# Splitting a modulation vector's sums between TensorE and VectorE at the start of a two-block transformer kernel

## The chip, the cores and the metric

One core of one Trainium2 chip runs the whole program. The metric is the device time of one execution in microseconds, as a median over runs; times within the program are counted from the first instruction of the profiled execution.

## What is computed

The reference runs two blocks of two layers each over 256 positions of width 1024. What matters here is its very beginning:

```python
c_act = jax.nn.silu(c)                                   # (1, 1024)
mod = c_act @ ada_w[l] + ada_b[l]                        # (1, 6144): six vectors of 1024
sh1, sc1, g1, sh2, sc2, g2 = jnp.split(mod, 6, axis=-1)
h = rmsnorm(x, norm_mix[l]) * (1.0 + sc1) + sh1
proj = h @ w_in[l]                                       # columns 512 to 1024 (a_v) are computed first
```

Nothing of the first layer's projection can begin before `sc1` and `sh1` are there, and each of them is a product of a vector of 1024 with a matrix of 1024 x 1024 (4 MB in float32). The rest (the mixer, a retrieval feed-forward network, a second block) follows from `h`.

## The kernel before

The inputs are float32. A projection's operands are each split into a rounded part `hi` and a difference `lo`, and three TensorE products of them are added. ScalarE makes `hi` (line 153), VectorE makes `lo` (line 154, recorded under its helper, line 81).

`first_norm` (line 745) makes `h` for the first layer. The matrix rows for `sc1` (group 1) and then `sh1` (group 0) come in 8 chunks each of 128 rows x 1024 columns, 512 KB, numbered 0 to 15 in this text. A ring of 7 buffers takes them: two tiles `ada_raw` and five slices of `more`. Each `part` (line 267) issues one transfer on SP's queue and one VectorE instruction that multiplies the chunk by one element of `cact` per partition and adds it to `ada_acc` (line 279 for a group's first chunk, line 282 for the others). Each `fin` (line 284) then adds up the partitions on TensorE, with `ada_acc` as the stationary operand and a column of ones moving:

```python
for j in range(8):
    pe.matmul(ps[:, j:j + 1], lhsT=st[g][:, j * 128:j * 128 + 128], rhs=ones, start=True, stop=True)
store = lambda: tt(MOD[l][:, g * 8:g * 8 + 8], ps[:, 0:8], C("ada_b", l * 48 + g * 8, 8), ALU.add)
```

The profile records each of these matmuls as two passes. I call the 16 passes of 8 such matmuls a set.

Meanwhile ScalarE takes the sums of squares of `X` (line 204), VectorE makes the reciprocal roots, ScalarE scales the rows (`xn`, line 760), and TensorE transposes them into four PSUM banks (`turn`, line 396, recorded at line 223). When both groups are there, ScalarE turns the banks into `hT_hi` with scale and shift (line 417), 8 instructions; VectorE (line 434) and, for the second half, ScalarE (line 432) make the full value `hfull`, and VectorE takes `hT_lo` from it (line 436). I call this the turn. The first projection starts on it: `Lead.rounded` (line 568) multiplies the first six rows of 128 of the weights, for which three weight chunks of 512 KB (two rows of 128 each) are loaded and split beforehand, chunks 0 and 1 ahead of the turn and chunk 2 in it. `Lead.small` (line 574) and `proj_half` (line 602) follow.

Within `first_norm` the orders of TensorE, VectorE and ScalarE are those in which the program is written (`tc.manual_schedule`). SP's queue issues transfers in order: a transfer into a ring buffer waits until the buffer's last reader is done, and all transfers behind it wait with it.

Of the kernel before, what the change touches and what calls it, by code (L numbers as in the profile page):

```python
# [8 lines left out]
F32 = mybir.dt.float32  # L9
F32R = mybir.dt.float32r  # L10
# [37 lines left out]
def kernel(ctx: ExitStack, tc: tile.TileContext, x, cols, ada_w, w_in, gm_wt, gm_vnorm, w_out,  # L48
# [214 lines left out]
    def ada_tasks(l, groups, acc, ring=None, name="ada", late=None, late_groups=(), halved=False, fetched=None):  # L263
        tasks = []
        st = {"n": 0}

        def part(g, k):
            src = ada_source(l, g, k)
            if fetched:
                raw = fetched(l, g, k)  # L270
            elif ring:
                raw = ring[st["n"] % len(ring)]
                st["n"] += 1
                sy.dma_start(raw, src)
            else:
                raw = load(src)
            if k == 0:
                st[g] = acc(g)
                ts(st[g], raw, cact[:, 0:1], None, ALU.mult)
                return  # L280
            for c in [slice(0, 512), slice(512, 1024)] if halved else [slice(0, 1024)]:
                ve.scalar_tensor_tensor(st[g][:, c], raw[:, c], cact[:, k:k + 1], st[g][:, c], ALU.mult, ALU.add)

        def fin(g):
            ps = bank("ta" if g in late_groups else name)
# [3 lines that stand above are left out]
            if g in late_groups:  # L289
                return store  # L290
            store()

        for g in groups:
            for k in range(8):
                tasks.append(lambda g=g, k=k: part(g, k))
            (late if g in late_groups else tasks).append(lambda g=g: fin(g))
        return tasks
# [79 lines left out]
    class Norm:  # L377
# [38 lines left out]
                else:  # L416
                    se.activation(d, src, AF.Identity, bias=self.shift[:, k:k + 1], scale=g)

        def lo(self, t, q):
            hi, lo = self.hT  # L420
            p = self.pieces(t)[4 * q:4 * q + 4]
            if self.shift is None:
                for k, src, c in p:
                    ve.scalar_tensor_tensor(lo[:, k, c], src, self.g[:, k:k + 1], hi[:, k, c].bitcast(F32), ALU.mult, ALU.subtract)
                return
            n = 4 if self.apart else 2
            for i in range(0, len(p), n):
                w = self.scr.tile([128, 512], F32, name="hfull", tag="hfull", bufs=1)
                for j, (k, src, c) in enumerate(p[i:i + n]):
                    d = w[:, j * 512 // n:(j + 1) * 512 // n]  # L430
                    if q:
                        se.activation(d, src, AF.Identity, bias=self.shift[:, k:k + 1], scale=self.g[:, k:k + 1])
                    else:
                        ts(d, src, self.g[:, k:k + 1], self.shift[:, k:k + 1], ALU.mult, ALU.add)
                d, c = slice(4 * q + i, 4 * q + i + n), p[i][2]
                tt(lo[:, d, c], w.rearrange("p (a b) -> p a b", a=n), hi[:, d, c].bitcast(F32), ALU.subtract)
# [308 lines left out]
    def first_norm(scr, hT, acc, ring):  # L745

        E = mybir.EngineType
        n = Norm(scr, lambda: gain1(0, 1, "norm_mix", "g_mix"), MOD[0][:, 0:8])
        n.hT = hT
        tasks = ada_tasks(0, (1, 0), acc, ring, "ta")  # L750
        src = paired(w_in[0, :, 512:1024])
        with tc.manual_schedule(engines={E.PE, E.DVE, E.Activation}):
            tasks[0]()
            for t in range(T):
                x_sumsq(t, X[:, t, :], strm.tile([128, 1024], F32, name="junk", tag="raw", bufs=3))
            r = rsqrt(sums[:, :, 0, 0], T, 1.0 / D)
            for t in range(T):
                parts[t] = [None, 0, None]
                xn = strm.tile([128, D], F32, name="xn", tag="raw", bufs=3)
                se.activation(xn, X[:, t, :], AF.Copy, scale=r[:, t:t + 1])  # L760
                n.turn(xn, t)
            for f in tasks[1:8] + tasks[9:12] + tasks[8:9]:
                f()
            n.prepare(0)
            for f in tasks[12:17]:
                f()
            ws = halves(0, src(0)) + halves(1, src(1))
            tasks[17]()
            for t in range(T):
                n.hi(t)  # L770
            n.lo(1, 0)
            ws += halves(2, src(2))
            n.lo(1, 1)
            cur["lead"] = ld = Lead(hT, ws, "sv", 1)
            for t in range(T):
                ld.parts(t)
            for i in range(len(ws)):
                for t in range(T):
                    ld.rounded(t, i)
            for t in range(T):  # L780
                ld.small(t)
# [927 lines left out]
```

## Time and profile before

| | us |
|---|---|
| runs | 2322.08, 2322.60, 2324.01 |
| median | 2322.6 |
| profiled execution, its own time | 2323.63 |
| its span, first to last instruction | 2321.8 |
| TensorE busy in the span | 2255.4 (97%) |
| VectorE busy | 1760.9 (76%) |
| ScalarE busy | 1198.8 (52%) |

The profiled execution is 1.0 us above the median, and 1.8 us of its time lie outside the span. The shares are means over the whole program; the stage in question is the first 36 us, 1.6% of it, in which the shares are others. PE is TensorE's matmul row and PEld its loading of stationary operands, DVE is VectorE, ACT is ScalarE, SP the queue that issues the transfers.

### The profile page before, as it was taken

The numbers are of one execution on the slowest core, as the hardware profiler recorded it, in microseconds if no ns is written. First come the engines' busy times: TensorE is split into PE (matmuls) and PEld (weight loads), VectorE is DVE, ScalarE is ACT, GpSimd is POOL, SyncE is SP. The second block draws the span as 40 slices with busy tenths as digits, with TensorE's granted clock in tenths as the row PEclk, the third lists the DMA queues.
The fourth block names the chain that finished last, engine by engine and source line by source line (L and its number), as shares of the span: only waits on it lengthen the run. The fifth ranks groups of instructions, "written<-read, shape, count | busy, mean of one in ns | idle before, by whom it ended". The sixth has DMA issues, their size and how long they took to land.

```text
span 2321.8 us, 39096 instructions
## 1 busy us (share of the span) xinstructions
PE 2255.4 (97%) x14953; PEld 2017.1 (87%) x14953; DVE 1760.9 (76%) x3277; ACT 1198.8 (52%) x1925; POOL 12.3 (1%) x36
## 2 busy tenths in 40 slices
PE   5999999999999999999999999999999999999998
PEld 4889999999887888888999999998888877987796
DVE  7875999999867777656489899996755666577556
ACT  4655545554444445466445555545444554654454
POOL 0000000000000000000000000000000000000000
PEclk8999999999999999999999999999999999999999
DMA  8845655544588887543455554447666673443552
GB/s 320 272 144 162 184 180 173 160 152 153 171 273 289 280 294 220 169 150 118 155 157 182 182 157 162 150 149 230 224 186 189 199 226 104 130 135 117 175 154 82
DMA packets 122029, 424.12 MB, mean 183 GB/s; under 512 B 14433, under 2 KB 15841, under 8 KB 121842
## 3 DMA queue, kind: packets, MB, share of 16 engines
q1 hardware_dynamic: 121842, 421.63, 57.2%
q8 instruction: 117, 1.92, 0.3%
q14 instruction: 70, 0.57, 0.1%
HBM read 420.53 MB, written 1.05 MB: 182 GB/s over the span
## 4 chain that ended last, share of the span: by engine, by line
PE 82%; DVE 10%; DMA 3%; ACT 2%; issue 2%; SPq 0%; DVEq 0%; ACTq 0%; POOL 0%
PE op L1048 10%; PE op L1050 9%; PE op L1049 9%; PE up L228 9%; PE up L230 9%; PE up L229 9%; DVE lo L81 3%; PE pc L230 3%; PE pc L228 3%; PE pc L229 3%; DVE Wx L81 2%; PE gg L958 2%; PE op L238 1%; PE op L241 1%; PE op L239 1%
## 5 line engine op out<-in xcount | busy, mean ns | idle before, releaser
L81 DVE TENSOR_TENSOR lo<-raw,hi 128x1024 fp32r<-128x1024 f32 x686 | 835.6, 1222 | 326.4 <-ACT hi L153 325.2
L153 ACT ACTIVATE hi<-raw 128x1024 fp32r<-128x1024 f32 x686 | 720.1, 1052 | 266.0 <-PE pc L229 75.5
L230 PE MATMUL up<-hT_hi,lo 128*128 128x256 f32 x2048 | 580.9, 284 | 5.0 <-DVE lo L81 4.8
L228 PE MATMUL up<-hT_hi,hi 128*128 128x256 f32 x2048 | 585.0, 286 | 0.0
L229 PE MATMUL up<-hT_lo,hi 128*128 128x256 f32 x2048 | 579.2, 283 | 0.0
L230 PEld LDWEIGHTS up<-hT_hi,lo 128*128 128x128 f32 x2048 | 392.4, 192 | 8.5 <-DVE lo L81 8.3
L229 PEld LDWEIGHTS up<-hT_lo,hi 128*128 128x128 f32 x2048 | 392.7, 192 | 0.0
L228 PEld LDWEIGHTS up<-hT_hi,hi 128*128 128x128 f32 x2048 | 392.3, 192 | 0.0
L1050 PE MATMUL op<-hi,lo 128*128 128x512 f32 x976 | 385.6, 395 | 2.7 <-DVE lo L81 2.7
L1048 PE MATMUL op<-hi 128*128 128x512 f32 x976 | 386.2, 396 | 0.2
L1049 PE MATMUL op<-lo,hi 128*128 128x512 f32 x976 | 385.2, 395 | 0.0
L1050 PEld LDWEIGHTS op<-hi,lo 128*128 128x128 f32 x976 | 183.0, 187 | 49.1 <-DVE lo L81 4.6
L1048 PEld LDWEIGHTS op<-hi 128*128 128x128 f32 x976 | 183.0, 188 | 45.0 <-DVE Wx L81 1.1
L1049 PEld LDWEIGHTS op<-lo,hi 128*128 128x128 f32 x976 | 183.0, 188 | 44.3
L228 PE MATMUL pc<-hT_hi,hi 128*128 128x256 f32 x568 | 160.9, 284 | 0.4 <-ACT hi L153 0.4
L230 PE MATMUL pc<-hT_hi,lo 128*128 128x256 f32 x568 | 160.7, 284 | 0.4 <-DVE lo L81 0.2
L229 PE MATMUL pc<-hT_lo,hi 128*128 128x256 f32 x568 | 160.7, 283 | 0.0
L990 ACT ACTIVATE up<-up 128x256 f32<-128x256 f32 (+31 forms) x140 | 37.7, 269 | 207.1 <-PE up L230 199.6
L153 ACT ACTIVATE hi<-Wy 128x256 fp32r<-128x256 f32 x120 | 50.1, 418 | 162.2 <-PE op L1049 162.1
L993 ACT ACTIVATE Wy<-up 128x256 f32<-128x256 f32 (+1 forms) x120 | 46.2, 385 | 167.1 <-PE up L230 167.0
L153 ACT ACTIVATE hi<-Wx 128x256 fp32r<-128x256 f32 x124 | 51.2, 415 | 129.2 <-PE op L1049 123.3
L228 PEld LDWEIGHTS pc<-hT_hi,hi 128*128 128x128 f32 x568 | 108.9, 192 | 1.4 <-ACT hi L153 1.3
(437 smaller groups left out, 3136.0 us busy)
## 6 DMA issues: line engine op xcount, KB each, us to landing
raw<-in_peer_ut_dram SPq DMA_DIRECT2D x256, 512.0 KB, 3.7
raw<-in_peer_v_dram SPq DMA_DIRECT2D x256, 512.0 KB, 4.3
Wx<-in_ada_w_dram SPq DMA_DIRECT2D x56, 512.0 KB, 5.5
raw<-in_even_w_dram SPq DMA_DIRECT2D x42, 512.0 KB, 4.1
raw<-in_w_in_dram SPq DMA_DIRECT2D x40, 512.0 KB, 4.4
raw<-in_peer_wq_dram SPq DMA_DIRECT2D x32, 512.0 KB, 4.0
raw<-in_odd_w_in_dram SPq DMA_DIRECT2D x32, 512.0 KB, 4.4
ada_raw<-in_ada_w_dram SPq DMA_DIRECT2D x30, 512.0 KB, 5.2
```

The costliest lines, as they stand in the source:

```text
L81: return ve.tensor_tensor(out, a, b, op)
L153: se.activation(hi, raw, AF.Copy)
L228: pe.matmul(dst, lhsT=wh[:, c0:c0 + 128], rhs=hh[:, k, :], start=first, stop=False, skip_group_check=True)
L229: pe.matmul(dst, lhsT=wh[:, c0:c0 + 128], rhs=hl[:, k, :], start=False, stop=False, skip_group_check=True)
L230: pe.matmul(dst, lhsT=wl[:, c0:c0 + 128], rhs=hh[:, k, :], start=False, stop=last, skip_group_check=True)
L238: pe.matmul(d, lhsT=a, rhs=wh[:, g * n:g * n + n], start=first, stop=False, **mk)
L958: pe.matmul(ps[:, a, q * 128:q * 128 + 128], lhsT=B[:, n // 2, :, n % 2], rhs=side[:, n // 2, :, n % 2], start=side is A and q == 0, stop= ...
L990: se.activation(ps[:, :P], ps[:, :P], AF.Gelu_apprx_tanh)
L993: se.activation(row(b)[:, P:], ps[:, P:256], AF.Gelu_apprx_tanh)
L1048: pe.matmul(d, lhsT=a, rhs=vh[:, s], start=first, stop=False, **mk)
L1049: pe.matmul(d, lhsT=a, rhs=vl[:, s], start=False, stop=False, **mk)
L1050: pe.matmul(d, lhsT=c, rhs=vh[:, s], start=False, stop=last, **mk)
```

## The change

Only `first_norm` and an argument of `Norm.lo` change. Chunks with an odd number within their group are multiplied on TensorE directly, with the chunk as the stationary operand and one column of `cact` moving, into the group's PSUM bank, where the products add up. Chunks with an even number are summed on VectorE as before, and after the sixth chunk of a group their sum goes into the same bank by `ones`. The `mod` addition comes when chunk 7 of the group has been multiplied. A ring buffer is filled again when its chunk has been used, by either engine.

The transposes stand after chunk 3's use. The first weight chunk is requested after chunk 6's use, that is between the requests for chunks 13 and 14; the other two after chunk 14's. Weight chunk 0 is split ahead of the turn, chunks 1 and 2 within it.

```diff
--- before.py
+++ after.py
@@ -416,7 +416,7 @@
                 else:
                     se.activation(d, src, AF.Identity, bias=self.shift[:, k:k + 1], scale=g)
 
-        def lo(self, t, q):
+        def lo(self, t, q, only=None):
             hi, lo = self.hT
             p = self.pieces(t)[4 * q:4 * q + 4]
             if self.shift is None:
@@ -424,7 +424,7 @@
                     ve.scalar_tensor_tensor(lo[:, k, c], src, self.g[:, k:k + 1], hi[:, k, c].bitcast(F32), ALU.mult, ALU.subtract)
                 return
             n = 4 if self.apart else 2
-            for i in range(0, len(p), n):
+            for i in range(0, len(p), n) if only is None else only:
                 w = self.scr.tile([128, 512], F32, name="hfull", tag="hfull", bufs=1)
                 for j, (k, src, c) in enumerate(p[i:i + n]):
                     d = w[:, j * 512 // n:(j + 1) * 512 // n]
@@ -747,30 +747,89 @@
         E = mybir.EngineType
         n = Norm(scr, lambda: gain1(0, 1, "norm_mix", "g_mix"), MOD[0][:, 0:8])
         n.hT = hT
-        tasks = ada_tasks(0, (1, 0), acc, ring, "ta")
-        src = paired(w_in[0, :, 512:1024])
+        order = [(g, k) for g in (1, 0) for k in range(8)]
+        src = lambda kk: w_in[0, kk * 256:kk * 256 + 256, 512:1024].rearrange("(a p) c -> p a c", p=128)
+        banks, sum_of = {}, {}
+
+        def fetch(m):
+            if m < len(order):
+                sy.dma_start(ring[m % len(ring)], ada_source(0, *order[m]))
+
+        def products(g, lhs, rhs, last):
+
+            first = g not in banks
+            if first:
+                banks[g] = bank("ta")
+            for j in range(8):
+                pe.matmul(banks[g][:, j:j + 1], lhsT=lhs[:, j * 128:j * 128 + 128], rhs=rhs, start=first and j == 0,
+                          stop=last, skip_group_check=True)
+
+        def use(m):
+
+            g, k = order[m]
+            raw = ring[m % len(ring)]
+            if k % 2:
+                products(g, raw, cact[:, k:k + 1], k == 7)
+            elif k == 0:
+                sum_of[g] = acc(g)
+                ts(sum_of[g], raw, cact[:, 0:1], None, ALU.mult)
+            else:
+                ve.scalar_tensor_tensor(sum_of[g], raw, cact[:, k:k + 1], sum_of[g], ALU.mult, ALU.add)
+                if k == 6:
+                    products(g, sum_of[g], ones, False)
+            fetch(m + len(ring))
+            if k == 7:
+                tt(MOD[0][:, g * 8:g * 8 + 8], banks[g][:, 0:8], C("ada_b", g * 8, 8), ALU.add)
+
+        def rounded(raw):
+            hi = strm.tile([128, 1024], F32R, name="hi", tag="hi")
+            se.activation(hi, raw, AF.Copy)
+            return hi
+
+        def rest(raw, hi):
+            lo = strm.tile([128, 1024], F32R, name="lo", tag="lo")
+            tt(lo, raw, hi.bitcast(F32), ALU.subtract)
+            return lo
+
         with tc.manual_schedule(engines={E.PE, E.DVE, E.Activation}):
-            tasks[0]()
+            for m in range(len(ring)):
+                fetch(m)
+            use(0)
             for t in range(T):
                 x_sumsq(t, X[:, t, :], strm.tile([128, 1024], F32, name="junk", tag="raw", bufs=3))
             r = rsqrt(sums[:, :, 0, 0], T, 1.0 / D)
+            for m in (1, 2, 3):
+                use(m)
             for t in range(T):
                 parts[t] = [None, 0, None]
                 xn = strm.tile([128, D], F32, name="xn", tag="raw", bufs=3)
                 se.activation(xn, X[:, t, :], AF.Copy, scale=r[:, t:t + 1])
                 n.turn(xn, t)
-            for f in tasks[1:8] + tasks[9:12] + tasks[8:9]:
-                f()
-            n.prepare(0)
-            for f in tasks[12:17]:
-                f()
-            ws = halves(0, src(0)) + halves(1, src(1))
-            tasks[17]()
-            for t in range(T):
-                n.hi(t)
-            n.lo(1, 0)
-            ws += halves(2, src(2))
+            for m in (4, 5, 6):
+                use(m)
+            raw0 = load(src(0), (128, 2, 512))
+            for m in range(7, 15):
+                use(m)
+                if m == 8:
+                    n.prepare(0)
+            raw1 = load(src(1), (128, 2, 512))
+            hi0 = rounded(raw0)
+            lo0 = rest(raw0, hi0)
+            use(15)
+            p = n.pieces(1)
+            turn_hi = lambda a, b: [se.activation(n.hT[0][:, k, c], ps, AF.Identity, bias=n.shift[:, k:k + 1],
+                                                  scale=n.g[:, k:k + 1]) for k, ps, c in p[a:b]]
+            turn_hi(0, 4)
+            n.lo(1, 0, (0,))
+            hi1 = rounded(raw1)
+            turn_hi(4, 8)
+            lo1 = rest(raw1, hi1)
+            raw2 = load(src(2), (128, 2, 512))
+            hi2 = rounded(raw2)
+            n.lo(1, 0, (2,))
+            lo2 = rest(raw2, hi2)
             n.lo(1, 1)
+            ws = halves(0, (hi0, lo0)) + halves(1, (hi1, lo1)) + halves(2, (hi2, lo2))
             cur["lead"] = ld = Lead(hT, ws, "sv", 1)
             for t in range(T):
                 ld.parts(t)
```

What this does to TensorE's queue, from its start (`ta` is a group's bank, `tp` the bank of a transpose, `sv` that of the first projection):

```order
+L764 MATMUL ta<-cact,ada_raw_109 128x1 x8
+L764 MATMUL ta<-cact,more 128x1 x8
 L223 MATMUL tp<-ident,xn 128x128 x16
-L287 MATMUL ta<-ones,ada_acc 128x1 x16
+L764 MATMUL ta<-cact,more 128x1 x8
+L764 MATMUL ta<-ones,ada_acc 128x1 x8
+L764 MATMUL ta<-cact,ada_raw_108 128x1 x8
+L764 MATMUL ta<-cact,more 128x1 x24
+L764 MATMUL ta<-ones,ada_acc 128x1 x8
+L764 MATMUL ta<-cact,ada_raw_109 128x1 x8
 L571 MATMUL sv<-hi,hT_hi 128x512
```

Where two reductions of 8 matmuls stood between the transposes and the first projection, there are now 80 matmuls, 16 of them ahead of the transposes.

VectorE's queue behind the reciprocal roots:

```order
-L282 SCALAR_TENSOR_TENSOR ada_acc<-ada_raw_109,cact,ada_acc 128x1024
-L282 SCALAR_TENSOR_TENSOR ada_acc<-more,cact,ada_acc 128x1024 x5
-L282 SCALAR_TENSOR_TENSOR ada_acc<-ada_raw_108,cact,ada_acc 128x1024
+L777 SCALAR_TENSOR_TENSOR ada_acc<-more,cact,ada_acc 128x1024 x3
+L81 TENSOR_TENSOR mod_101<-ta,col 128x8
 L85 TENSOR_SCALAR ada_acc<-ada_raw_109,cact 128x1024
-L282 SCALAR_TENSOR_TENSOR ada_acc<-more,cact,ada_acc 128x1024 x2
+L311 SCALAR_TENSOR_TENSOR g_mix<-mod_101,col 128x8
+L777 SCALAR_TENSOR_TENSOR ada_acc<-more,cact,ada_acc 128x1024 x2
+L777 SCALAR_TENSOR_TENSOR ada_acc<-ada_raw_108,cact,ada_acc 128x1024
```

The seven sums of the first group become three, and the addition that makes `mod` from TensorE's bank now stands ahead of the second group's first chunk.

ScalarE's queue around the turn (`hT_hi` is the turn, `hi<-raw` the rounding of a weight chunk):

```order
-L153 ACTIVATE hi<-raw 128x1024 x2
-L417 ACTIVATE hT_hi<-tp,mod_101,g_mix 128x256 x8
-L153 ACTIVATE hi<-raw 128x1024
+L786 ACTIVATE hi<-raw 128x1024
+L820 ACTIVATE hT_hi<-tp,mod_101,g_mix 128x256 x4
+L786 ACTIVATE hi<-raw 128x1024
+L820 ACTIVATE hT_hi<-tp,mod_101,g_mix 128x256 x4
+L786 ACTIVATE hi<-raw 128x1024
 L432 ACTIVATE hfull<-tp,mod_101,g_mix 128x256 x4
```

One rounding has moved from ahead of the turn into its middle.

## Rows read from the trace of the kernel before

**Rows 1.** The page, busy time by engine: us, share of the span, instructions.

```profile
PE 2255.4 (97%) x14953; PEld 2017.1 (87%) x14953; DVE 1760.9 (76%) x3277; ACT 1198.8 (52%) x1925; POOL 12.3 (1%) x36
```

**Rows 2.** The chain of waits, 8 to 37 us: start, us, what.

```profile
20.35 1.30 DVE ada_acc L282
...
21.69 3.59 PE ta L287 x16
...
30.86 1.30 DVE ada_acc L282
...
32.20 3.59 PE ta L287 x16
...
36.01 0.57 ACT hT_hi L417
```

**Rows 3.** Busy time by stretch; last three columns granted TensorE clock, DMA share, GB/s.

```profile
12.50:21.60 9.10, 3.65 (x16) 3.28 (x16) 8.88 (x9) 2.19 (x2) 0.00 (x0) 0.98 1.01 390
...
25.30:32.10 6.80, 0.00 (x0) 0.00 (x0) 6.62 (x8) 2.08 (x2) 0.00 (x0) 0.50 0.98 351
```

**Rows 4.** Timeline of TensorE: start, us, instruction; transposes and one-column passes.

```profile
13.84 3.65 PE L223 MATMUL tp<-ident,xn 128*128 128x128 f32 x16 [13.84 <-ACT xn L760]
...
147.50 1.03 PE L223 MATMUL tp<-ident,xn 128*128 128x128 f32 x8
...
149.75 3.63 PE L287 MATMUL ta<-ones,ada_acc 128*128 128x1 f32 x32
...
154.80 1.97 PE L223 MATMUL tp<-ident,xn 128*128 128x128 f32 x8 [1.42 <-DVE xn L85]
```

**Rows 5.** Busy time by stretch (as rows 3: PE, PEld, DVE, ACT, POOL, clock, DMA, GB/s).

```profile
21.70:25.20 3.50, 3.50 (x16) 3.48 (x16) 3.17 (x3) 0.00 (x0) 0.00 (x0) 0.50 1.02 376
32.20:35.70 3.50, 3.50 (x16) 3.49 (x16) 2.22 (x2) 0.00 (x0) 0.00 (x0) 0.50 0.67 207
35.80:41.60 5.80, 4.97 (x12) 3.91 (x13) 5.21 (x10) 5.11 (x10) 0.00 (x0) 0.50 0.99 395
...
149.80:153.30 3.50, 3.50 (x33) 3.49 (x31) 2.39 (x9) 0.72 (x2) 0.00 (x0) 1.00 0.36 136
...
154.50:157.70 3.20, 2.90 (x14) 2.90 (x15) 2.00 (x8) 2.18 (x5) 0.00 (x0) 0.50 0.00 0
```

**Rows 6.** SP's issues of chunks 1 and 14, 15, with chunks 1 and 15 to landing.

```profile
2.66 0.43 SPq L274 DMA_DIRECT2D ada_raw<-in_ada_w_dram  x1
...
ada_raw<-in_ada_w_dram SPq DMA_DIRECT2D x1, 512.0 KB, 7.3
...
21.66 0.99 SPq L274 DMA_DIRECT2D ada_raw<-in_ada_w_dram  x2
...
ada_raw<-in_ada_w_dram SPq DMA_DIRECT2D x1, 512.0 KB, 6.0
```

**Rows 7.** Timeline of ScalarE: the scaled rows and the turn.

```profile
12.55 2.19 ACT L760 ACTIVATE xn<-X,rs_y 128x1024 f32<-128x1024 f32 x2 [4.94 <-DVE rs_y L131]
...
36.01 3.75 ACT L417 ACTIVATE hT_hi<-tp,mod,g_mix 128x256 fp32r<-128x256 f32 x8 [3.88 <-DVE mod L81]
```

**Rows 8.** Timeline of VectorE: differences of weight chunks, and its part of the turn.

```profile
32.06 2.35 DVE L81 TENSOR_TENSOR lo<-raw,hi 128x1024 fp32r<-128x1024 f32 x2
...
37.07 0.99 DVE L86 TENSOR_SCALAR hfull<-tp,g_mix,mod 128x256 f32<-128x256 f32 x2 [0.43 <-ACT hT_hi L417]
38.10 0.69 DVE L81 TENSOR_TENSOR hT_lo<-hfull,hT_hi 128x512 fp32r<-128x512 f32 x1
```

**Rows 9.** The chain of waits, first projection: one matmul's step early and later.

```profile
40.41 0.43 PE sv L571
...
42.24 0.23 PE sv L572
```

**Rows 10.** Busy time by stretch after the stage (columns as rows 3).

```profile
44.80:60.00 15.20, 14.53 (x95) 12.70 (x94) 11.25 (x14) 9.34 (x10) 0.00 (x0) 1.00 0.89 294
60.00:100.00 40.00, 39.48 (x258) 34.91 (x257) 32.79 (x54) 26.26 (x33) 0.00 (x0) 1.00 0.84 283
100.00:150.00 50.00, 49.48 (x278) 41.95 (x277) 42.35 (x96) 30.11 (x47) 0.00 (x0) 1.00 0.56 190
```

## The prediction

> **What bounds the kernel now.** Over the whole span TensorE is the bound [rows 1], but the change lies in the first 36 us, before the projections begin, so I read that stage by itself, first in the chain of waits. There the links are VectorE's modulation sums, one per chunk at 1.30 us, then a reduction of 16 TensorE passes (8 matmuls by `ones`, two passes each) of 3.59 us, twice, and after the second (32.20 + 3.59 = 35.79 us) ScalarE's turn of the activations begins at 36.01 [rows 2]. 35.79 is the time that the change must beat.
>
> Next, what stands beside that chain. In the two stretches of sums VectorE is busy 8.88 of 9.10 and 6.62 of 6.80 us, and the DMA engines' share is 1.01 and 0.98 [rows 3]. So the sums run hardly behind the transfers, and less work on VectorE alone can win little. The last chunk's transfer takes 6.0 us from its issue at about 22.3 (the second of two that go out in 21.66 to 22.65), so it is in SBUF at 28.3 [rows 6]. In the change the first weight chunk (512 KB, at 390 GB/s [rows 3] 1.3 us) goes ahead of the last two chunks, so 29.6 is an estimate of the earliest landing. Even if TensorE had nothing else left, 29.6 + 3.59 = 33.2, which is 2.6 us before 35.79. That is about the most that the plan can win at this price of a pass.
>
> Then what one TensorE set costs. A set is 16 passes with a 128x128 f32 stationary operand and one column moving. The reductions before are this same form, so the new products are priced by them: 3.59 us at a granted clock of 0.50 (1.2 GHz) [rows 2, 5], and 3.63 for 32 passes, so 1.82 us a set, at 1.00 (2.4 GHz) [rows 4, 5]. Everything hangs on which level the new stream gets.
>
> **The change, part by part.**
>
> *Removed from VectorE:* 8 multiply-adds of 1.30 us, 10.4 us. They were on the chain, but what takes their place is longer, so I count no gain of their own.
>
> *Added to TensorE:* 8 sets for the odd chunks; the 2 sets by `ones` stay (over the even chunks alone) and so do the 16 transposes. TensorE takes its work in order: product 1, product 3, the transposes, product 5, sum 6, products 7, 9, 11, 13, sum 14, product 15. That is 10 sets and the transposes. It starts when chunk 1 has landed: issued at 2.66, landed 7.3 us later, 9.96 [rows 6]. The scaled rows for the transposes are done at 12.55 + 2.19 = 14.7 [rows 7], before TensorE gets to them.
>
> *Which clock.* The transposes at 13.84 take 3.65 us for 16, 228 ns each. At 147.50 they take 1.03 / 8 = 129 ns, and at 154.80, with 0.50 granted, 1.97 / 8 = 246 [rows 4, 5]. So the engine starts at the lower level, though the clock column reads near 1.00 until 21.6 (0.98 over [rows 3]). Then the reductions: TensorE busy without a gap for 3.50 us at 21.70 and again at 32.20, clock 0.50 throughout. After the second come 512-wide products, and the clock stays 0.50 until 41.6 [rows 5]. After the 32 one-column passes at 149.80, which follow dense products at 1.00, the clock is at 0.50 from 154.50 on, so they ended in a fall and not in a stay [rows 4, 5]. No stretch of one-column passes in this trace is followed by a rise of its own. So I price all 10 sets at 3.59.
>
> *The sum of the stage.* 9.96 + 2 x 3.59 + 3.65 + 8 x 3.59 = 49.5 us, against 35.79: +13.7. TensorE never runs dry in it. Chunks 14 and 15 are fetched late, since the transfer queue is in order and waits for product 7 (20.79 + 3 x 3.59 = 31.6) to free a buffer. At 6.0 us each they are there by about 38; VectorE needs chunk 14 by 42.3 - 1.3 = 41.0 at the latest, and product 15 starts at 45.9. VectorE itself waits for product 7 with the `mod` addition, and chunk 8's, 10's and 12's sums are queued behind it: 31.6 + 0.2 + 4 x 1.3 = 37 at the latest, also in time. The weight loads behind these fetches land by about 40, before they are read.
>
> *What could give some back.* Before, the clock column read 1.00 for 21.25 - 17.49 = 3.8 us after the transposes had ended; the end is 13.84 + 3.65 [rows 4], and a mean of 0.98 over 9.1 us [rows 3] puts 0.02 x 9.1 / 0.5 = 0.36 us at 0.50 ahead of 21.6. If the transposes bring such a spell again, now with sets behind them, 3.8 us hold 2.1 sets at 1.82 instead of 3.59: 3.7 us back, +10.0. The transposes now stand between one-column passes, and nothing before shows whether the spell comes there. I take the middle, **+11.9**, and keep 10.0 and 13.7 as ends.
>
> *The turn of the activations.* Before, weight chunks 0 and 1 were split ahead of the turn; now only chunk 0 is. ScalarE does 4 of the 8 turns (3.75 / 2 = 1.9), then the rounding of chunk 1 (about 1.1, as `xn` [rows 7]), the other 4 turns (1.9) and the rounding of chunk 2 (1.1): 6.0 us. VectorE puts two differences of 1.2 (2.35 / 2) among two pairs of `hfull` (0.99) and two of `hT_lo` (0.69), with one sum of the next modulation group between [rows 8]. From the turn's start, chunk 1 is whole at about 4.2 and chunk 2 at 7.8. TensorE wants them, at 4 matmuls for each row of 128, at 0.43 us at first and 0.23 after the rise [rows 9], at about 4.5 and 7.0. Chunk 1 costs nothing, chunk 2 some 0.6: **+0.6**. Below, nothing; above, the whole rounding and difference, 2.3.
>
> *After it.* The same matmuls follow, on a TensorE that is idle 40.00 - 39.48 = 0.5 us in 60 to 100 and as much in 100 to 150, and 0.7 in 44.8 to 60 [rows 10]. So a later start can be won back by 1.7 us at the very most, and I take nothing. Queues differ a little in the first mixer; I put 1.5 us on either side for that.
>
> **Sum:** 11.9 + 0.6 = +12.5. The profiled execution took 2323.63, so 2336.1; it lies 1.03 above the median of the runs shown (2322.6), so against the median **2335**.
>
> **The rivals.**
>
> *The stream lifts the clock by itself (not slower).* Mechanism: TensorE is busy almost without a gap from 9.96, the clock goes to 1.00 some 5.1 us after, as it did for the projection that starts at 36.6 and sees its rise after 41.6 [rows 5], and sets cost 1.82 from then on. By 15.1 product 1 is done and product 3 to 43%; then 0.57 x 1.82 = 1.0, transposes 16 x 0.129 = 2.1, and products 5, 7, 9, 11, 13 with sum 6 at 1.82: 29.1. The transfers now end last: chunk 14 issued after product 7 at 23.7, there at 29.7, 1.3 on VectorE, then two sets: 34.6, a gain of 1.2. The projection would run at 1.00 at once, but waits for the third weight chunk (7.8 of the turn) and ends its leading products about 0.4 later than now: 2322. Against it: the two gapless reductions at 0.50 and the fall after 149.80 [rows 5]. For it: none of these stretches is as long as the stream would be. It decides if the column reads 1.00 by the time of product 5.
>
> The Trainium skill's page "TensorE: Matmul & The Clock Gate", section "Why this matters for your kernels", says that keeping TensorE continuously busy brings it to the higher level, and by it this rival would be the forecast. This trace agrees for the projection's 512-wide products and does not for the reductions at 21.70 and 32.20, which were gapless at 0.50.
>
> *Repeated spells.* The spell after the transposes comes again, two or three times in the stream, each worth 3.7: 13.7 - 7.4 + 0.6 gives 2329.5, with three 2326. For it: one spell did come. Against: only the transposes preceded it.
>
> *The change does not bind.* The scheduler could put the sets where TensorE is free and the end is DMA: -2.6, no more than 2320. Against: the order of TensorE's queue is pinned in this stage, and 10 sets and the transposes are 39.5 us of work in one queue at 0.50, however early they start.
>
> **How the numbers follow.** Slow stream with at most one spell: 0.80, from 2322.6 + 10.0 + 0 - 1.7 - 1.5 = 2329 to 2322.6 + 13.7 + 2.3 + 1.5 = 2340. Repeated spells: 0.07. The stream lifts the clock: 0.10, 2320 to 2324. Does not bind: 0.03. The range 2328 to 2340 takes in the first case and the two-spell half of the second, some 0.84. A measurement of this kernel tells about 0.2% from no change, 4.6 us: faster means below 2318.0, slower above 2327.2. Faster 0.03 (tails of the last two cases), same 0.13, slower 0.84.
>
> **What would show it.** In the profile after: products of 3.6 us a set at a granted 0.50 from about 10 us, TensorE busy to about 46 to 50 us, the second `mod` addition there instead of at 35.8, VectorE idle for more than half of 20 to 45, DMA share well under 1 in 25 to 45. The rest of the kernel is shifted and else alike. It is wrong if the sets take 1.8 us, or if the first projection starts before 40 us, or if the shift at 60 us is not still there at 160.

## The result, and the profile after

The change takes **2335.55 us** (median of five runs, 2334.47 to 2337.79) where the kernel before, run beside it, takes 2322.69 (median of six): a ratio of **1.0052**, interval [1.004, 1.0063], so slower by about 12 us. A sixth run of the change took 3158 us at a mean granted clock of 0.65, is unlike every other run here, and is left out. The profiled execution took 2334.47, its span is 2332.8, 11.0 longer than that of before. The prediction was 2335, in 2328 to 2340.

The page's busy times after the change, to be held against [rows 1]:

```profile
PE 2279.2 (98%) x15081; PEld 2042.9 (88%) x15081; DVE 1751.0 (75%) x3269; ACT 1199.3 (51%) x1925; POOL 13.9 (1%) x36
```

TensorE has gained 128 instructions (8 sets of 16 passes) and 23.8 us of busy time, VectorE has lost 8 instructions and 9.9 us. The work moved as the diff says. What it cost is in the chain of waits over the first 52 us (start, us, what):

```profile
2.66 6.26 DMA ada_raw<-in_ada_w_dram
...
9.06 6.96 PE ta L764 x32
16.02 3.11 PE tp L223 x16
19.12 24.40 PE ta L764 x128
...
43.55 0.18 DVE mod L81
...
50.05 1.15 DVE lo L81
...
51.24 0.50 PE sv L572
```

Where [rows 2] alternate between VectorE's sums and two reductions, now nearly all is TensorE's: two sets, the transposes, eight sets in series, 34.5 us from 9.06 to 43.53. The second `mod` addition starts at 43.55. Before, the second reduction ended at 35.79 and the turn began at 36.01 [rows 2], with the addition at 35.81 between them. So **the stage ends 7.7 us later**.

This difference hides a part of the cost, since the two executions did not start alike. VectorE's first use of chunk 0 and the second `mod` addition in the profile of before, and the first use of chunk 0 in the change's, where the addition is the one at 43.55:

```profile
8.83 0.75 DVE L85 TENSOR_SCALAR ada_acc<-ada_raw,cact 128x1024 f32<-128x1024 f32 x1 [7.90 <-DMA ada_raw<-in_ada_w_dram]
...
35.81 0.17 DVE L81 TENSOR_TENSOR mod<-ta,col 128x8 f32<-128x8 f32 x1 [1.40 <-PE ta L287]
```

```profile
7.77 0.75 DVE L85 TENSOR_SCALAR ada_acc<-ada_raw,cact 128x1024 f32<-128x1024 f32 x1 [6.84 <-DMA ada_raw<-in_ada_w_dram]
```

Chunk 0 landed 1.1 us earlier in the change's profile. Counted from its first use, the stage takes 26.98 us before and 35.78 in the change, so **8.8 us longer**. I call this the stage's length. It hardly differs between executions of one kernel: the repeats at the end of the experiments give 26.99 (`e11`) and 35.79 (`e12`).

TensorE's timeline in the stage, one line for each tile of a set or row of sets (start, us, instruction; a set is x16; the bracket is idle time and what ended it):

```profile
9.06 3.55 PE L764 MATMUL ta<-cact,ada_raw 128*128 128x1 f32 x16 [9.06 <-DMA ada_raw<-in_ada_w_dram]
12.47 3.55 PE L764 MATMUL ta<-cact,more 128*128 128x1 f32 x16
15.88 3.25 PE L223 MATMUL tp<-ident,xn 128*128 128x128 f32 x16
18.96 1.84 PE L764 MATMUL ta<-cact,more 128*128 128x1 f32 x16
20.67 2.36 PE L764 MATMUL ta<-ones,ada_acc 128*128 128x1 f32 x16
22.89 3.55 PE L764 MATMUL ta<-cact,ada_raw 128*128 128x1 f32 x16
26.31 10.38 PE L764 MATMUL ta<-cact,more 128*128 128x1 f32 x48
36.55 3.55 PE L764 MATMUL ta<-ones,ada_acc 128*128 128x1 f32 x16
39.96 3.55 PE L764 MATMUL ta<-cact,ada_raw 128*128 128x1 f32 x16
...
51.24 0.50 PE L572 MATMUL sv<-lo,hT_hi 128*128 128x512 f32 x1 [0.42 <-DVE lo L81]
```

A set takes 3.55 by itself, and the next one begins 3.41 after it (12.47 - 9.06). Only the two sets behind the transposes take 1.84 and 2.36. From 9.06 to the last set no line has idle time before it. Busy time by stretch (PE, PEld, DVE, ACT, POOL, then granted clock, DMA share, GB/s):

```profile
17.00:20.80 3.80, 3.80 (x30) 3.80 (x28) 0.00 (x0) 0.00 (x0) 0.00 (x0) 1.00 1.03 415
20.80:24.40 3.60, 3.60 (x25) 3.60 (x24) 0.00 (x0) 0.00 (x0) 0.00 (x0) 0.66 0.78 254
24.40:28.00 3.60, 3.60 (x18) 3.60 (x19) 1.52 (x4) 0.00 (x0) 0.00 (x0) 0.50 0.74 231
...
35.00:38.70 3.70, 3.70 (x19) 3.70 (x19) 0.00 (x0) 0.00 (x0) 0.00 (x0) 0.50 0.46 174
38.70:42.30 3.60, 3.60 (x18) 3.60 (x19) 0.00 (x0) 0.00 (x0) 0.00 (x0) 0.50 0.00 0
```

TensorE is busy in every microsecond, and the clock stays at 0.50 (1.2 GHz) from 24.4 to the end of the stage, as in the reductions of [rows 5]. VectorE does nothing in 17 to 24.4 and in 35 to 42.3, and DMA falls to 0.46 and 0.00, where [rows 3] had 1.01 and 0.98.

Behind the stage the shift changes little for long: the first projection's leading products end at 54.95 instead of 46.58 (+8.4), and the second norm's turn starts at 163.98 instead of 155.52 (+8.5). At 205 us, where the feed-forward network of this layer begins to choose its rows, it is +9.5, at the end +11.0.

### The profile page after: what moved, and what is told of

It is laid out like the page before. It is cut to its first block, busy times and chain, and to the rows that moved or that the text cites. A ratio compares the mean times of both kernels' runs of the same rounds, so it can differ in the third digit from the quotient of the medians.

```text
span 2332.8 us, 39343 instructions
## 1 busy us (share of the span) xinstructions
PE 2279.2 (98%) x15081; PEld 2042.9 (88%) x15081; DVE 1751.0 (75%) x3269; ACT 1199.3 (51%) x1925; POOL 13.9 (1%) x36
## 4 chain that ended last, share of the span: by engine, by line
PE 83%; DVE 10%; DMA 3%; ACT 2%; issue 2%; SPq 0%; DVEq 0%; ACTq 0%
PE op L1107 10%; PE op L1109 10%; PE op L1108 10%; PE up L228 9%; PE up L230 9%; PE up L229 9%; DVE lo L81 3%; PE pc L230 3%; PE pc L228 3%; PE pc L229 3%; DVE Wx L81 2%; PE gg L1017 2%; PE op L238 1%; PE op L241 1%; PE op L239 1%
## 5 line engine op out<-in xcount | busy, mean ns | idle before, releaser
L230 PEld LDWEIGHTS pc<-hT_hi,lo 128*128 128x128 f32 x568 | 108.7, 192 | 2.0 <-DVE lo L81 1.9
```

What stands on the lines that cost most here:

```text
L230: pe.matmul(dst, lhsT=wl[:, c0:c0 + 128], rhs=hh[:, k, :], start=False, stop=last, skip_group_check=True)
```

## The experiments

My theory: the stage lasts as long as TensorE's sets take in series, because a stream of one-column passes does not lift the clock from 0.50. Rivals: the number of sets doesn't matter, and the order of the fetches, the late weights or VectorE's queue holds the stage up; or the stream is slow for another reason than the clock. Twelve kernels ran in three groups, each beside the kernel before, which took 2324.1 (`e1` to `e4`), 2326.07 (`e5` to `e8`, on another chip) and 2324.94 us (`e9` to `e12`). So totals are compared by their ratio to before. "The stage's end" is the start of the second `mod` addition: 35.81 before, 43.55 in the change. It moves with the landing of chunk 0, so the stage's length is given where two profiles are compared.

### No set moved to TensorE, everything else as changed (`e1_all_vector`)

```diff
-            if k % 2:
-                products(g, raw, cact[:, k:k + 1], k == 7)
-            elif k == 0:
+            if k == 0:
...
-                if k == 6:
-                    products(g, sum_of[g], ones, False)
+                if k == 7:
+                    products(g, sum_of[g], ones, True)
```

> The changed kernel with all 16 chunks summed on VectorE again, 2 reduction sets on TensorE; its fetch order, the weight splits within the turn and everything else stay. Theory (the 8 added sets at a granted clock of 0.50 are the loss): the second mod addition falls back from 43.6 us to about 37 (35.8 before, and 1.2 for the first weight chunk's difference, which now stands ahead of the last sum on VectorE), the turn costs 0.6 more than before: 2324 to 2325. Rival (the fetch order and the late splits of the weights are the loss): it stays at 2332 or above.

Measured: 2329.72, ratio 1.0019 [1.0011, 1.0028], stage's end at 40.16, 3 us later than I expected. Chunk 0 was first used at 8.94, so the stage's length is 31.22: 4.6 us shorter than the change's and 4.2 longer than before. VectorE's timeline shows why:

```profile
25.41 0.17 DVE L81 TENSOR_TENSOR mod<-ta,col 128x8 f32<-128x8 f32 x1 [3.67 <-PE ta L764]
...
34.08 1.22 DVE L81 TENSOR_TENSOR lo<-raw,hi 128x1024 fp32r<-128x1024 f32 x1
35.21 1.28 DVE L775 SCALAR_TENSOR_TENSOR ada_acc<-ada_raw,cact,ada_acc 128x1024 f32<-128x1024 f32 x1
40.16 0.17 DVE L81 TENSOR_TENSOR mod<-ta,col 128x8 f32<-128x8 f32 x1 [3.67 <-PE ta L764]
```

The first `mod` addition stands ahead of the second group's sums in VectorE's queue and holds them for a whole reduction (3.67), and a weight difference of 1.22 stands ahead of the last sum. So the changed order has a cost of its own, which in the change does not add to the sets: VectorE waits for TensorE there anyway. The change is worse by the 4.6 us that the sets take on top.

### VectorE's queue put back too (`e5_vector_queue`)

On `e1`: the first `mod` addition goes behind chunk 10's sum, the weight difference behind the last sum.

```diff
                 use(m)
-                if m == 8:
+                if m == 10:
+                    mod(1)
                     n.prepare(0)
...
-            lo0 = rest(raw0, hi0)
-            use(15)
+            use(15, lambda: los.append(rest(raw0, hi0)))
...
```

> The first experiment (all chunks on VectorE in the changed kernel's order) with two instructions moved in VectorE's queue: the first group's mod addition behind chunk 10's sum instead of right behind chunk 7's, and the first weight chunk's difference behind chunk 15's sum instead of ahead of it. Theory (what the first experiment kept of the loss is VectorE idle 3.7 us ahead of the mod addition, and 1.2 of the difference): the second mod addition at 36 us, as before, and 0.6 for the weight splits in the turn: 2323 to 2324.5 beside 2322.6. Rival (the fetch order with a weight chunk between chunks 13 and 14 is what it kept): no change, second mod addition at 40, 2327 or more.

Measured: 2328.45, ratio 1.0011 [1.0002, 1.0019], stage's end at 35.07. VectorE's two `mod` additions:

```profile
24.56 0.17 DVE L81 TENSOR_TENSOR mod<-ta,col 128x8 f32<-128x8 f32 x1 [0.36 <-PE ta L764]
...
35.07 0.17 DVE L81 TENSOR_TENSOR mod<-ta,col 128x8 f32<-128x8 f32 x1 [2.53 <-PE ta L764]
```

The first one now waits 0.36 instead of 3.67. Chunk 0 was first used at 8.09, so the stage's length is 26.98, as before. The 4.2 us to `e1` are these two positions (of the 5.1 between the two ends, 0.9 is the earlier landing); the order of the fetches costs nothing here. The total is nevertheless 0.1% above before, more than I expected. About 1.1 us of that arise in the first projection's leading products, which take 9.04 us to the start of the last 12 instead of 7.95; the rest is not traced.

### Four sets instead of eight (`e2_four_sets`)

```diff
-            if k % 2:
+            if k in (3, 7):
                 products(g, raw, cact[:, k:k + 1], k == 7)
```

> Only chunks 3 and 7 of each group are multiplied on TensorE, the other six are summed on VectorE: 4 product sets and 2 reductions instead of 8 and 2. Theory: TensorE's queue is no longer the bound; now VectorE waits for the first group's last product (about 25 us) before it may sum the second group's six chunks (0.75 + 5 x 1.3 = 7.3), then a reduction and a product at 3.4 each: the second mod addition at 39 to 40.5, 2326 to 2328.5. Rival (each set taken off gives back its 3.41): 13.6 less than the change, 2323.

Measured: 2331.87, ratio 1.003 [1.0018, 1.0042]. Its last set is done at 36.25 + 3.55 = 39.8, as expected; the total lies above the expectation even with the 1.5 us by which before is slower in this group. VectorE's first `mod` addition, and then three rows of TensorE's timeline:

```profile
25.33 0.17 DVE L81 TENSOR_TENSOR mod<-ta,col 128x8 f32<-128x8 f32 x1 [7.39 <-PE ta L764]
```

```profile
15.02 3.65 PE L223 MATMUL tp<-ident,xn 128*128 128x128 f32 x16
18.47 3.41 PE L764 MATMUL ta<-ones,ada_acc 128*128 128x1 f32 x16
...
32.81 3.57 PE L764 MATMUL ta<-ones,ada_acc 128*128 128x1 f32 x16 [4.11 <-DVE ada_acc L777]
```

Four sets fewer give back 3.7 us and not four steps of 3.41: VectorE waits 7.39 for the first group's last product, and later TensorE waits 4.11 for VectorE's sum. Here the two queues waiting for each other set the end. That the number of sets sets it in the change is shown by the next run and not by this one.

There is also a surprise: the same transposes, and by the durations no spell at 1.00 behind them. (The clock column is of no use here. It reads 1.00 over this whole stage, though every set takes 3.4.) What decides whether the spell comes stays open.

### All sixteen chunks on TensorE (`e10_all_tensor`)

```diff
-            if k % 2:
-                products(g, raw, cact[:, k:k + 1], k == 7)
...
+            products(g, raw, cact[:, k:k + 1], k == 7)
             fetch(m + len(ring))
...
```

> All 16 chunks multiplied on TensorE with one column moving, no sums on VectorE and no reductions: 16 sets instead of the change's 10. Theory (sets at 0.50 stand one behind the other in TensorE's queue, 3.41 us each): TensorE starts at 7.8 with chunk 0 and ends its sets 16 x 3.41 + 3.3 later, less 3.4 if the transposes bring the clock up for a while: second mod addition at 62 to 66 us, 18 to 22 after the change's 43.6, 2353 to 2358. Rival (a stream that long lifts the clock by itself, or the transfers are the bound): under 2345.

Measured: 2355.38, ratio 1.0136 [1.0121, 1.015], stage's end at 62.83. That is the change's 43.55, plus six more sets at the step of 3.41 (20.5), less the 1.2 us by which chunk 0 lands before chunk 1: 62.8. From its TensorE timeline, the last two rows of sets, back to back:

```profile
38.76 17.20 PE L764 MATMUL ta<-cact,more 128*128 128x1 f32 x80
55.82 6.96 PE L764 MATMUL ta<-cact,ada_raw 128*128 128x1 f32 x32
```

17.20 us for five sets, still 3.4 each after more than 45 us of nothing but sets and transposes. The level came up once, behind the transposes, for some 3.5 us, and from 32 to 62 us the clock column reads 0.50 without a break: the length of the stream does not help.

### The same sets, 64 equal columns wide (`e3_wide`)

The moving operand is the same column 64 times; one of the 64 results is read.

```diff
-                pe.matmul(banks[g][:, j:j + 1], lhsT=lhs[:, j * 128:j * 128 + 128], rhs=rhs, start=first and j == 0,
+                pe.matmul(banks[g][:, j * 64:j * 64 + 64], lhsT=lhs[:, j * 128:j * 128 + 128], rhs=rhs.to_broadcast([128, 64]), start=first and j == 0,
                           stop=last, skip_group_check=True)
...
```

> The changed kernel with a moving operand of 64 equal columns instead of one in every set (each column gives the same sum, one of them is read). Theory (a set costs 3.4 because the stream of one-column passes leaves the clock at 0.50, and the loading of the stationary operand sets the pace): the clock reads 1.00 from the first or second product on and stays there, a set takes 1.7 to 1.9, the second mod addition falls to 33 to 35 us, set by the transfers, and the projection starts at 1.00: 2319 to 2323. Rival (the price of a set has nothing to do with the clock, or wider operands cost their columns): sets at 3.4 or more, 2336 or above.

Measured: 2331.29, ratio 1.0029 [1.0019, 1.004], stage's end at 38.33. From TensorE's timeline:

```profile
12.90 3.62 PE L764 MATMUL ta<-cact,more 128*128 128x64 f32 x16
16.32 3.14 PE L223 MATMUL tp<-ident,xn 128*128 128x128 f32 x16
19.29 1.90 PE L764 MATMUL ta<-cact,more 128*128 128x64 f32 x16
...
24.60 5.52 PE L764 MATMUL ta<-cact,more 128*128 128x64 f32 x48
31.80 3.08 PE L764 MATMUL ta<-ones,ada_acc 128*128 128x64 f32 x16 [1.67 <-DVE ada_acc L777]
34.67 3.62 PE L764 MATMUL ta<-cact,ada_raw 128*128 128x64 f32 x16
```

and its busy time by stretch:

```profile
24.60:30.10 5.50, 5.50 (x50) 5.38 (x49) 3.43 (x5) 0.99 (x1) 0.00 (x0) 1.00 0.94 325
30.10:31.80 1.70, 0.03 (x2) 0.01 (x1) 1.34 (x2) 0.07 (x1) 0.00 (x0) 1.00 1.01 389
31.80:38.20 6.40, 6.40 (x32) 6.30 (x32) 1.07 (x1) 0.00 (x0) 0.00 (x0) 0.55 0.70 241
```

This is the clearest test of the cause. At 0.50 a set of 64 columns costs what one of 1 column costs (3.62 against 3.55), but this stream keeps the clock at 1.00 (2.4 GHz) from 19.3 to 30.1 and does its sets in 1.90, where the change fell back to 0.50 at 22.0. What is shown is that these sets hold the level that came with the transposes, not that they bring it: the two ahead of the transposes took 3.6 each. Then the stream has become too fast for the transfers: chunk 14 is requested only when product 7 frees its buffer and lands at 30.4, TensorE idles 1.67 us for its sum, the clock falls at 32.5, and the last two sets take 3.08 and 3.62. I had expected 33 to 35 for the stage's end, and 2319 to 2323 for the total, and left that wait out.

### Four wide sets, better queues, filled or not (`e6`, `e7`, `e9`)

All three combine `e2`'s four sets, `e3`'s width and `e5`'s first position, request the weight chunks behind all 16 matrix chunks, and split weight chunk 1 earlier. So against the change several things differ at once; `e7` and `e9` differ by the fillers alone. `e6_composite` also keeps TensorE from idling, by 512-wide products of `ident` with each chunk that has no set of its own; `e7_comp_no_extra` has none; `e9_paced` has four, near the end of the stage. From `e6`, and from `e9`:

```diff
+            if k not in (3, 7):
+                for c in (0, 512) if m < 3 else (0,):
+                    pe.matmul(keep, lhsT=ident, rhs=raw[:, c:c + 512], start=True, stop=True)
```

```diff
+            for c in {12: (0,), 13: (0, 512), 14: (0,)}.get(m, ()):
+                pe.matmul(keep, lhsT=ident, rhs=raw[:, c:c + 512], start=True, stop=True)
```

> Chunks 3 and 7 of each group on TensorE, with a moving operand of 64 equal columns; for each other chunk one product of 512 columns of it with the identity, whose result is not read (two for chunks 0 to 2), so that TensorE has dense work as the chunks land; the first mod addition behind chunk 10's sum; the weight loads behind all 16 chunks; weight chunk 0 split ahead of the turn, chunk 1 beside it. Theory (clock and queue positions are the loss, the transfers are the floor): sets at 1.8 throughout, the second mod addition at 31.5 to 33 us, the projection at 1.00 from its start: 2316 to 2319.5. Rival (extra dense work on TensorE delays the sets, or the clock falls anyway): second mod addition at 36 or later, 2323 or more.

> The kernel of the run before without the extra products. Theory: TensorE is idle between its six sets, the clock falls to 0.50 in the gaps, the last two sets cost 3.4 each and the projection begins at 0.50: second mod addition at 36 to 37 us, 2321.5 to 2324. Rival (the division of the chunks alone brings the gain): second mod addition at 33 or earlier, 2319 or less.

> The composite without extra work, plus four products of 512 columns with the identity (results not read), of chunk 12, twice chunk 13 and chunk 14, in the gap that TensorE had between product 11 and the last reduction. Theory (there the composite lost the clock in an idle gap of 3.7 us, and the last two sets and the projection's first products went at 0.50): the clock stays at 1.00, the last two sets take 1.8 to 1.9, the second mod addition at 32.5 to 34 us instead of 36.3, and the projection leads off at 1.00: 2 to 5 us less than the composite without them, and at or under the kernel before on the same chip (ratio 0.998 to 1.000). Rival (the extra products come in the way of the reduction, as in the composite with more of them): 36 us or later, ratio 1.001 or more.

Measured: `e6` 2327.64, 1.0013 [1.0004, 1.0022], stage's end at 37.29; `e7` 2329.75, 1.0012 [1.0003, 1.002], at 36.28; `e9` 2324.29, 0.9997 [0.9989, 1.0006], at 33.55. In `e6` the clock held at 1.00 to the projection and every set took 1.89 to 1.95, but the extra products cost 0.86 us each (the first four, at 0.50, 1.64), and the queue that they lengthen ended later than I had expected (31.5 to 33). `e7`'s last sets on TensorE:

```profile
29.16 3.67 PE L764 MATMUL ta<-ones,ada_acc 128*128 128x64 f32 x16 [3.67 <-DVE ada_acc L777]
32.63 3.62 PE L764 MATMUL ta<-cact,ada_raw 128*128 128x64 f32 x16
```

and `e9`'s:

```profile
24.74 2.79 PE L781 MATMUL ta<-more,ident 128*128 128x512 f32 x6
27.89 1.12 PE L781 MATMUL ta<-ada_raw,ident 128*128 128x512 f32 x2 [0.35 <-DMA ada_raw<-in_ada_w_dram]
29.28 2.00 PE L764 MATMUL ta<-ones,ada_acc 128*128 128x64 f32 x16 [0.26 <-DVE ada_acc L779]
31.11 1.95 PE L764 MATMUL ta<-cact,ada_raw 128*128 128x64 f32 x16
```

In `e7` TensorE idles 3.67 us and both sets cost 3.6; in `e9` four products of 512 columns fill that hole and both cost 2.0. That is the price of the clock at the end of the stage, at the same place with the same sets. `e9` is 12 us (0.5%) better than the change and equal to before. Its stage is 2.3 us shorter than before (24.68 from chunk 0's first use), and that does not show in the total: against `e11`, the kernel before in the same group, it is 0.7 us ahead at the second norm's turn and 0.8 behind at the third's, some 990 us in. Where that goes is not traced.

### The kernel before, with fillers (`e8_before_extra`)

Two 512-wide products for each of the chunks 9 to 15, ahead of the two reductions, so that these find the clock at 1.00.

```diff
+            if keep is not None and st["n"] > 9:
+                for c in (0, 512):
+                    pe.matmul(keep, lhsT=ident, rhs=raw[:, c:c + 512], start=True, stop=True)
```

> The kernel before, unchanged but for two products of 512 columns of each of the chunks 9 to 15 with the identity, whose results are not read. Theory (the price of a set and of the projection's first products is the clock): the clock reads 1.00 from about 25 us to the projection, the second reduction takes 1.8 instead of 3.6, the projection starts at 1.00 and is held up for the third weight chunk: 1.8 to 4 us less, 2318.5 to 2321. Rival (a reduction's price has nothing to do with the clock): reduction 3.6, 2322 or more.

Measured: 2330.8, ratio 1.002 [1.0011, 1.0029], stage's end at 38.86. From TensorE's timeline:

```profile
20.02 6.75 PE L279 MATMUL ta<-more,ident 128*128 128x512 f32 x8 [3.01 <-DMA more<-in_ada_w_dram]
26.61 1.84 PE L290 MATMUL ta<-ones,ada_acc 128*128 128x1 f32 x16
...
36.98 1.84 PE L290 MATMUL ta<-ones,ada_acc 128*128 128x1 f32 x16
```

Both one-column reductions take 1.84 as expected, since they follow 512-wide products. But the fillers ran at 0.50 at first (6.75 us for 8 passes) and pushed the first reduction to 26.61, and VectorE waited 4.03 us for it, so that the total rose by 0.2% where I had expected a gain. A filler ahead of a reduction is itself in the queue.

### The weight chunks split earlier (`e4_early_split`)

Chunks 1 and 2 are rounded and split ahead of the turn; otherwise as changed.

```diff
             lo0 = rest(raw0, hi0)
+            hi1 = rounded(raw1)
+            lo1 = rest(raw1, hi1)
+            raw2 = load(src(2), (128, 2, 512))
+            hi2 = rounded(raw2)
+            lo2 = rest(raw2, hi2)
             use(15)
...
```

> The changed kernel with weight chunks 1 and 2 split into rounded part and difference ahead of the last product, where ScalarE and VectorE are idle, instead of within the turn. Theory: the projection no longer waits for the third weight chunk, 0.6 us less, 2336. Rival (the late splits are several us of the loss): 2333 or less.

Measured: 2336.25, ratio 1.0055 [1.0042, 1.0068]. From the first projection's first product to the start of its last 12 leading products it took 8.30 us instead of the change's 8.59 (7.95 before): 0.3 of the 0.6 that I had expected. In the total nothing of it shows.

### Before and change once more (`e11_before_again`, `e12_change_again`)

Both kernels unedited, for what two executions of one kernel differ by.

> The kernel before, unchanged, as one of the runs: what two samples of the same kernel differ by on this chip. Both theories: ratio 1.000 within 0.001; a larger one would say how far the ratios of the other runs can be read.

> The changed kernel, unchanged, on the same chip as the experiments. Theory: ratio 1.004 to 1.006 again, its runs in two groups some 3 us apart, those with a mean granted clock of about 0.988 (a spell at 1.00 after the transposes) below those with 0.993 (no spell, where the column has no reading before the first rise). Rival (the two groups were chance): one group.

Measured: `e11` 2324.46, ratio 1.0001 [0.9992, 1.001], stage's end at 34.72. `e12` 2336.01, ratio 1.0048 [1.0035, 1.0061], at 43.94. The change's loss repeats in this second set of runs. `e12`'s profiled execution had the spell (its set behind the transposes took 1.84) and was nevertheless one of its longer ones, 2338.62; so the spread of the change's runs is not the spell's coming or not, as I had supposed. And `e11` against the profile of before shows what a profile can't tell: the same kernel was 1.26 us ahead at 205 us and 0.7 behind at the end.

## Why the prediction was right

**The clock: right, and it decides.** The step that priced all sets at the lower level from the reductions before [rows 5] held: 0.50 from 24.4 to 43.5. The rival in which the stream lifts the clock is false for one-column passes: in the change the level even fell, at 22.0, in a stream without a gap, and in `e10` it stayed at 0.50 for 30 us. Passes of 64 columns held the level once it was there (`e3`), and that they bring it is not shown. The rule of the Trainium skill's page "TensorE: Matmul & The Clock Gate", section "Why this matters for your kernels", that a TensorE kept continuously busy gets the higher level, does not agree with the change's trace: without a gap from 22.89 to 43.5, at 0.50. It agrees with `e3` from 19.3 to 30.1, where wide sets without a gap kept 1.00. Ahead of the result I had only the two reductions of 3.5 us each to set against that rule; the 20 us of the change are the test of it.

**One spell: right as an end of the range.** I took 11.9, the middle between none (13.7) and one (10.0). One came, in the change's profile, in `e4` and in `e12`, and not a second, so the rival of repeated spells is out; and the last one, that the sets would go where TensorE is free and the transfers end the stage, is out by the gapless timeline.

**The price of a set: 5% too high.** The term that was mis-sized is the set at 3.59. That is how long a lone set takes; in series the next one starts 3.41 after it. Eight sets at the lower level are 8 x 0.18 = 1.4 us less. And product 1 started at 9.06, not 9.96, since the transfers landed earlier in that execution: 0.9 less, which is luck and no property of the change. With these, 10.0 - 1.4 - 0.9 = 7.7, which is what was measured. Two smaller misses nearly cancel in it: the transposes took 3.1 instead of 3.65, and the spell did two sets in 3.93 instead of 2 x 3.59, so it gave back 3.3 and not 3.7. The reductions of [rows 2] stand alone and cannot show a step; only sets behind one another do.

**The turn: right.** A cost of +0.6 was predicted for the third weight chunk; the shift grew from 7.7 to 8.4 over the turn, and TensorE waited 0.42 for that chunk's difference at 51.24.

**Nothing won back: right, but a remainder that was put at 0 is not settled.** The shift was about the same at 164 us. Then it grew by 1.1 to 205 us, and there the clock is at work, but not the change. Ten microseconds around the second norm, in the profile of before, of the change and of `e11`:

```profile
151.50:161.50 10.00, 8.58 (x62) 8.50 (x63) 6.51 (x22) 5.46 (x12) 0.00 (x0) 0.83 0.18 55
```

```profile
160.00:170.00 10.00, 8.59 (x53) 8.50 (x53) 6.54 (x22) 5.43 (x12) 0.00 (x0) 0.66 0.19 55
```

```profile
149.00:159.00 10.00, 8.59 (x52) 8.51 (x52) 6.55 (x22) 5.41 (x12) 0.00 (x0) 0.66 0.18 55
```

A mean of 0.66 over 10 us is 6.8 us at 0.50, and 0.83 is 3.4. `e11` is the kernel before, unedited, and it has the longer low stretch too: it was 2.6 us ahead of the other profile of before at this norm and 1.3 ahead at 205 us. So this part of the shift is a difference between two executions of one kernel. The last 1.5 us of the profiled execution's +11.0, and the 2 more of the medians, arise behind 205 us, where `e11` shows that an unchanged kernel drifts by 2.

So that +12.5 met +12.9 (of the medians) so closely is luck. Stage and turn came to 8.4, 4.1 under the forecast, or to 9.4 when counted from chunk 0's first use. Some 3.5 to 4.5 us of the loss arise later, for which I had put 0 with 1.5 on either side, and no run here shows where. The mechanism and its place in TensorE's queue are shown; the sum owes its closeness to two errors that leaned opposite ways.

**Queues: too little said.** I counted VectorE's wait at the first `mod` addition as harmless, and in the change it is. `e1` and `e5` show that it is worth, with the weight difference ahead of the last sum, 4.2 us as soon as TensorE no longer covers it. Whoever takes the sets back out of this change keeps that cost.

**Not tried:** eight wide sets with chunk 14's buffer freed earlier, and the transposes moved later, between the sets. `e9` alone drew level with before; no version beat it.

## What to carry to other kernels

Before moving sums from a busy VectorE to an idle-looking TensorE, price the TensorE work at the clock that its own form of instruction held in the trace, in series and not by itself: here eight sets at 3.41 replaced eight sums at 1.30. Before comparing times between two profiles, count them from an event that both share, here the first use of the first chunk. If short passes must run ahead of the dense work, widen them or fill the holes between them, read the granted clock, and look at what the faster engine waits for next. An order changed beside the main edit has its price even when the main edit hides it: undo one without the other.

## What the runs showed of the hardware that I had not expected

A stream without a gap is not enough for the higher clock. One-column passes fell from 1.00 to 0.50 at 22.0 in the change and stayed there for 20 us, and for 30 us in `e10`; sets of 64 equal columns held 1.00 for 10.8 us in `e3`, at the same price for a set at the lower level (3.62 against 3.55). The level was lost 0.7 us behind a hole of 1.67 us in `e3` and inside one of 3.67 in `e7`, while holes of 0.35 and 0.26 in `e9` did not end it.

A spell at 1.00 followed the 16 transposes in the change (1.84 for the next set) but not in `e2` (3.41). And the clock column reads 1.00 from the start, although the first sets and transposes go at half speed (3.41 to 3.55 a set, 228 ns a transpose); in `e2` it reads 1.00 to the end of the stage, with every set at 3.4. So the level of the first stretch has to be read from durations.
